# Differential attention: each group's output kept as features by queries, turned only for the squares of its norm; one more pair of key tiles as split products; split rings five deep

## The chip, the core and the metric

One core of a Trainium2 chip runs the kernel. The metric is the device time of one execution in microseconds (us). Five engines work from queues of their own and in order: PE (TensorE, matrix products and transposes; PEld is its weight load), DVE (VectorE), ACT (ScalarE), POOL (GpSimd) and SP (SyncE, which here only issues transfers). They meet at semaphores. PE writes its results to PSUM, a small memory of eight banks, each 512 numbers of four bytes wide on each of 128 partitions; DVE and ACT read it, POOL does not. SBUF is the larger on-chip memory.

## The reference

The kernel computes one layer of a diffusion backbone for two streams: 256 context tokens ("prompt", p) and 2048 latent tokens ("sample", s), 1024 wide. Per stream: a modulated norm, one projection to q, k, v and Fourier channels, differential attention in 4 heads, a Fourier mixing, an output projection with a gated residual, and a squared-ReLU MLP. What the change touches is the attention's end:

```python
s = jnp.einsum('bqhmd,bkhmd->bhmqk', qblk, k) * scale      # m: two halves of a head
p = jax.nn.softmax(s, axis=-1)
a = p[:, :, 0] - lam * p[:, :, 1]
attn = jnp.einsum('bhqk,bkhe->bqhe', a, v)                 # e: 128 features of a head
...
a = rms_norm(attn, subln_g) * (1.0 - lam_init)             # norm over the 128 features
mix = jnp.concatenate([a.reshape(b, n, 512), four], axis=-1) @ w_out
x = x + gate1 * mix
```

Sample queries see 2560 keys (512 cached and 2048 new), prompt queries their own 256. All is float32. Where a product is marked `float32r`, PE takes its operands in a shorter form; the kernel keeps the accuracy by splitting an operand into a high and a low part (`h`, `l`) and adding three products: high by high, high by low, low by high.

## The kernel before

The program has three stages that matter here, by the profile's clock: projection and Fourier mixing to about 520 us, **attention** to 1243 us, then the **output projection** to about 1470 us, and the MLP (done as seven products in place of eight, with sums of blocks) to the end.

*Attention.* Four heads, and in each head 8 groups of 256 sample queries (two blocks `j` of 128), 32 groups in all; one prompt group per head is threaded between them. The order of everything is written out: `add(t, fn)` puts a step at a nominal time, the list `ev` is sorted by time, and each engine gets its instructions in that order. Nominal time runs in slots `T` of 5 units `u`; a group takes four slots, and three groups are in flight at different depths.

- *Scores.* In each slot, five `fill`s (L1080, 2 products of 512 columns each) write five score banks `S`; DVE takes the row maximum of each (`rowmax`, L1085) and the maximum over the five (`comb`, L1088); ACT then takes five exponentials (`exp`, L1104). There are 5 `S` banks, so the fill of the next slot waits for the exponential that frees its bank.
- *Combine.* POOL forms p0 - lam * p1 (L1119, L1120), on 128 x 2560 per block.
- *Turning.* `tr` (L1135) transposes two key tiles of both blocks into one of two banks `pt`: four transposes, named by the first tile `kb` (0, 2 ... 18). ACT copies the bank to SBUF (`ah`, L1142; it is also the high part), DVE subtracts that copy from the bank (`al`, L1147; the low part). A bank `pt` is free when both have read it. Slots q = 0 to 3 of a group turn the tiles 0, 2 / 4, 6, 8 / 10, 12 / 14, 16, 18.
- *Values.* One slot later, `mul` multiplies by V into columns 0 to 255 of one bank, `po`: six split products of 256 columns per `kb` (`mm3`, L94 to L96). The tiles in `FULL`, 4 and 14, are done as plain float32 products with unsplit values instead (L1161), have no `al`, and the first quarter of tile 14 is done early (`mul_part`, L1168).
- *Output of a group.* `o1` (ACT) copies `po` columns 0 to 255 to SBUF, features by queries; `o2` (PE, L1176) transposes it into columns 256 to 511 of the same bank; `o3` (DVE, L1180) copies that to SBUF, queries by features; `o4` (ACT, L1186) takes the sums of squares; `o5` (DVE L1189, POOL L91) makes the factor of the norm; `o6` (POOL L1195) multiplies and SP stores it to `att` in DRAM, queries by features. For sample groups `o1` to `o6` stand at nominal 0, 0.4, 4.25, 8.5, 9.2 and 9.6 u after the group's last product.
- The two last groups are exceptions (`drain`, `last`): as no fills follow them, their transposes take turns over seven banks.

*Output projection.* `seq` walks 18 tiles of 128 tokens. For each, `mix` loads the attention rows (`am`), turns them back on PE (L1572, four transposes), ACT scales them with subln_g (L1573), DVE splits them (L1576, L1577), and `out_mm` does 2 x 24 products of 512 columns (L94 to L96) against the split weights from `w_split`. `finish` turns the normed result for the MLP (L248). For the first tile the turning is done at the end of the attention (`mix0_tr`, L1280).

Of the kernel before, what the change touches and what calls it, by code (L numbers as in the profile page):

```python
# [32 lines left out]
FULL = (4, 14)  # L33
# [8 lines left out]
def body(tc, a, out):  # L42
    nc = tc.nc
    ctx = ExitStack()
    with ctx:
# [16 lines left out]
        att = [scratch(f"att{i}", [P, 512]) for i in range(NT // P)]  # L62
# [46 lines left out]
        def setup_cond(pool, pps, rows):  # L109
# [8 lines left out]
            nc.vector.tensor_scalar_mul(cols[:, 96:97], cols[:, 96:97], 1.0 - LAM_INIT)  # L118
# [870 lines left out]
        with ExitStack() as c3_:  # L989
# [49 lines left out]
            class Group:  # L1039
# [66 lines left out]
                def combine(self, j):  # L1106
# [5 lines left out]
                    nc.gpsimd.tensor_scalar(self.s0e[:, j:j + 1], tot[:, 0:1], tot[:, 0:1], EPS, op0=ALU.mult, op1=ALU.mult)  # L1112
# [25 lines left out]
                def ah(self, kb):  # L1138
                    full = kb in self.hd.vf
                    t = at.tile([P, 512], F32 if full else F32R, tag="af" if full else "ah", name=f"ah{self.nm}_{kb}", bufs=2 if full else 4)  # L1140

                    (nc.vector.tensor_copy if self.drain and kb == FULL[0] else nc.scalar.copy)(t, self.pt[kb])  # L1142
                    self.A[kb] = [t]

                def al(self, kb):
                    t = at.tile([P, 512], F32R, tag="al", name=f"al{self.nm}_{kb}", bufs=4)
# [23 lines left out]
                def o1(self):  # L1170
                    self.oT = self.op.tile([P, 256], F32, tag="oT", name=f"oT{self.nm}", bufs=1 if self.last else 2)
# [6 lines left out]
                def o3(self):  # L1178
                    self.o = self.op.tile([P, 256], F32, tag="o", name=f"o{self.nm}")
                    nc.vector.tensor_copy(self.o, self.po[:, 256:512])  # L1180

                def o4(self):
                    osq = self.op.tile([P, P], F32, tag="osq", name=f"osq{self.nm}", bufs=1)
                    self.oss = self.op.tile([P, 4], F32, tag="oss", name=f"oss{self.nm}")
                    for j in range(2):
                        nc.scalar.activation(osq, self.o[:, j * P:j * P + P], AF.Square, accum_out=self.oss[:, j:j + 1])  # L1186

                def o5(self):
                    nc.vector.scalar_tensor_tensor(self.oss[:, 0:2], self.oss[:, 0:2], 1.0 / P, self.s0e, op0=ALU.mult, op1=ALU.add)  # L1189
                    pow_mhalf(self.oss[:, 2:4], self.oss[:, 0:2], 2)  # L1190

                def o6(self):
                    for j in range(2):
                        c = slice(j * P, j * P + P)
                        nc.gpsimd.tensor_scalar(self.o[:, c], self.o[:, c], self.oss[:, 2 + j:3 + j], 0.0, op0=ALU.mult, op1=ALU.add)  # L1195
                        (nc.gpsimd if self.last else nc.sync).dma_start(att[self.hd.tok0 + self.g * 2 + j][:, self.hd.hc], self.o[:, c])

            class Prompt(Group):
# [21 lines left out]
                def combine(self, j):  # L1220
# [3 lines left out]
                    nc.gpsimd.tensor_scalar(self.s0e[:, j:j + 1], t[:, 2:3], t[:, 2:3], EPS, op0=ALU.mult, op1=ALU.mult)  # L1224
# [13 lines left out]
                def mul(self, j):  # L1238

                    (ah, al), V = self.A[0], self.hd.V  # L1240
                    n = 0
                    for t in range(2):
                        c = slice((t * 2 + j) * P, (t * 2 + j) * P + P)
                        for l, r in ((ah[:, c], V[:, t, 0, :]), (ah[:, c], V[:, t, 1, :]), (al[:, c], V[:, t, 0, :])):
                            n += 1
                            nc.tensor.matmul(PRO()[:, 256 + j * P:256 + j * P + P], l, r, start=False, stop=(n == 6), skip_group_check=True)

                def o3(self):
                    self.o = self.op.tile([P, 256], F32, tag="o", name=f"o{self.nm}")
                    nc.vector.tensor_copy(self.o, PRO()[:, 256:512])  # L1250


# [8 lines left out]
            def load_wout():  # L1261
# [9 lines left out]
                MIX0.extend((f32(ts[0])[:, 2 * D:2 * D + 512], f32(ts[2])[:, 4 * D:5 * D].rearrange("p (k t) -> p k t", t=P)))  # L1271
                nc.sync.dma_start(MIX0[1][:, 4:8, :], four[:, 0:P].rearrange("(k p) t -> p k t", p=P))

            def mix0_load():
                nc.sync.dma_start(MIX0[0], att[0])

# [855 lines left out]
```

## Time and profile before

| | |
|---|---|
| median of 3 runs | 2862.73 us (2862.22 to 2862.76) |
| span of the profiled execution, first to last instruction | 2861.4 us |
| PE, DVE, ACT, POOL busy | 99%, 71%, 54%, 38% of the span |
| granted TensorE clock, mean | 0.999 |
| one group of 256 queries in the attention | about 22.0 us, start of a part to the same start of the next group |
| one tile of the output projection | 12.25 us |

The profiled execution was not timed apart from its span; its span lies 1.3 us below the median of the timed runs. In a row of the timeline stand start, length, engine, line, operation, out<-in by the program's names, shape, a count where like instructions were merged, and in brackets the idle time ahead and who ended it. PE's lengths include the way through the array, so rows overlap; the cost of a product in a dense row is the distance between starts. In a row of groups, the two numbers behind the bar are busy time in total and the mean of one in ns, then the idle time ahead and its releasers.

### The profile page before, as it was taken

The numbers are of one execution on the slowest core, as the hardware profiler recorded it, in microseconds if no ns is written. First come the engines' busy times: TensorE is split into PE (matmuls) and PEld (weight loads), VectorE is DVE, ScalarE is ACT, GpSimd is POOL, SyncE is SP. The second block draws the span as 40 slices with busy tenths as digits, with TensorE's granted clock in tenths as the row PEclk, the third lists the DMA queues.
The fourth block names the chain that finished last, engine by engine and source line by source line (L and its number), as shares of the span: only waits on it lengthen the run. The fifth ranks groups of instructions, "written<-read, shape, count | busy, mean of one in ns | idle before, by whom it ended". The sixth has DMA issues, their size and how long they took to land.

```text
span 2861.4 us, 43224 instructions
## 1 busy us (share of the span) xinstructions
PE 2831.7 (99%) x15109; PEld 2455.9 (86%) x15109; DVE 2018.0 (71%) x3393; ACT 1548.2 (54%) x3505; POOL 1073.3 (38%) x890
## 2 busy tenths in 40 slices
PE   8999999999999999999999999999999999999999
PEld 5888888688888888888889999999998888888887
DVE  7767886898988989864477777778775354345554
ACT  4333323798989989853356565556555332333221
POOL 1211223798999989942223333333332000000000
PEclk9999999999999999999999999999999999999999
DMA  7776777421211212036767676667747464445663
GB/s 284 219 207 198 230 213 237 172 106 38 73 71 53 106 38 99 23 124 201 242 221 232 223 246 228 221 219 238 234 167 255 147 202 135 138 144 185 206 206 111
DMA packets 392780, 492.94 MB, mean 172 GB/s; under 512 B 26467, under 2 KB 306384, under 8 KB 389490
## 3 DMA queue, kind: packets, MB, share of 16 engines
q1 hardware_dynamic: 387136, 479.73, 50.9%
q0 software_dynamic: 1872, 7.28, 0.8%
q10 hardware_dynamic: 3554, 3.17, 0.4%
q8 instruction: 119, 1.95, 0.3%
q14 instruction: 99, 0.81, 0.1%
HBM read 312.58 MB, written 179.59 MB: 172 GB/s over the span
## 4 chain that ended last, share of the span: by engine, by line
PE 54%; DVE 1%; DMA 0%; ACT 0%; issue 0%; SPq 0%; POOL 0%; DVEq 0%; POOLq 0%
PE ps L94 8%; PE ps L95 8%; PE ps L96 8%; PE pB L1749 2%; PE pB L1747 2%; PE pB L1748 2%; PE pA L1748 2%; PE pC L1748 2%; PE pA L1749 2%; PE pC L1747 2%; PE pA L1747 2%; PE pC L1749 2%; PE po L94 2%; PE po L96 2%; PE po L95 2%; PE pD L1749 1%
## 5 line engine op out<-in xcount | busy, mean ns | idle before, releaser
L1085 DVE TENSOR_REDUCE mxs<-Ss 128x1 f32<-128x512 f32 x636 | 405.4, 686 | 65.5 <-PE Ss L1080 55.1
L1420 DVE TENSOR_TENSOR sl<-sr,sh 128x768 fp32r<-128x768 f32 x168 | 161.8, 964 | 331.5 <-ACT sh L1419 331.1
L1120 POOL TENSOR_TENSOR P0s<-P0s,P1s 128x1024 f32<-128x1024 f32 (+2 forms) x128 | 378.6, 2958 | 10.7
L1419 ACT CAST sh<-sr 128x768 fp32r<-128x768 f32 x168 | 140.6, 838 | 418.3 <-PE ps L95 418.3
L1789 POOL TENSOR_TENSOR gs<-g,g 128x384 f32<-128x384 f32 x48 | 69.7, 1452 | 468.5 <-ACT g L1759 418.9
L1104 ACT ACTIVATE P1s<-Ss,mxs 128x512 f32<-128x512 f32 x318 | 215.4, 694 | 36.3 <-DVE mxs L1088 35.3
L94 PE MATMUL pj<-wh,hh 128*128 128x512 f32 x576 | 228.8, 397 | 2.0 <-DVE hh L555 2.0
L94 PE MATMUL ps<-thT,sh 128*128 128x512 f32 x585 | 227.6, 389 | 0.0
L95 PE MATMUL ps<-tlT,sh 128*128 128x512 f32 x585 | 227.6, 389 | 0.0
L96 PE MATMUL ps<-thT,sl 128*128 128x512 f32 x585 | 227.6, 389 | 0.0
L95 PE MATMUL pj<-wl,hh 128*128 128x512 f32 x576 | 227.1, 394 | 0.5 <-DVE wl L516 0.5
L96 PE MATMUL pj<-wh,hl 128*128 128x512 f32 x576 | 225.6, 392 | 0.0
L1104 ACT ACTIVATE P0s<-Ss,mxs 128x512 f32<-128x512 f32 x318 | 214.3, 691 | 5.6 <-DVE mxs L1088 5.0
L1135 PE MATMUL pts<-ident,P0s 128*128 128x128 f32 x1280 | 191.7, 273 | 4.5 <-DVE als L1147 1.8
L1080 PE MATMUL Ss<-KS0s,Qs 128*128 128x512 f32 x636 | 190.1, 419 | 0.4 <-ACT P1s L1104 0.4
L1080 PE MATMUL Ss<-KS1s,Qs 128*128 128x512 f32 x636 | 188.7, 420 | 1.5 <-ACT P0s L1104 1.4
L1758 ACT ACTIVATE g<-uz 128x384 f32<-128x384 f32 x144 | 75.7, 526 | 200.2 <-DVE uz L1781 174.1
L1135 PEld LDWEIGHTS pts<-ident,P0s 128*128 128x128 f32 x1280 | 151.3, 140 | 35.9 <-issue 4.8
L1119 POOL TENSOR_SCALAR P1s<-P1s,tots 128x1024 f32<-128x1024 f32 (+2 forms) x128 | 171.9, 1343 | 5.8
L1147 DVE TENSOR_TENSOR als<-pts,ahs 128x512 fp32r<-128x512 f32 x256 | 165.9, 681 | 6.9 <-ACT ahs L1142 6.7
L94 PE MATMUL ps<-ophT,sh 128*128 128x512 f32 x423 | 164.7, 389 | 1.1 <-DVE uz L1781 1.1
L96 PE MATMUL ps<-ophT,sl 128*128 128x512 f32 x423 | 164.6, 389 | 0.0
(536 smaller groups left out, 8073.9 us busy)
## 6 DMA issues: line engine op xcount, KB each, us to landing
sr<-sd SPq DMA_DIRECT2D x84, 768.0 KB, 4.5
a<-in_w SPq DMA_DIRECT2D x184, 256.0 KB, 4.2
sd<-gs SPq DMA_DIRECT2D x192, 192.0 KB, 1.9
sd<-g SPq DMA_DIRECT2D x144, 192.0 KB, 2.1
wm<-in_w_mod SPq DMA_DIRECT2D x32, 512.0 KB, 5.2
Qs<-qd SPq DMA_DIRECT2D x32, 512.0 KB, 4.0
b<-in_w SPq DMA_DIRECT2D x64, 256.0 KB, 5.8
b<-tsum SPq DMA_DIRECT2D x64, 256.0 KB, 4.7
```

Source lines behind the costliest of these rows:

```text
L94: nc.tensor.matmul(ps, lh, rh, start=first, stop=False)
L95: nc.tensor.matmul(ps, lh, rl, start=False, stop=False)
L96: nc.tensor.matmul(ps, ll, rh, start=False, stop=last)
L1080: nc.tensor.matmul(S[:, :w], self.Q[:, x, m, j * P:j * P + P], self.hd.KS[m][:, b * 512:b * 512 + w], start=(x == 0), stop=(x == 1))
L1085: nc.vector.tensor_reduce(self.mx[j][:, m, b:b + 1], self.S[j, m, b], axis=AX.X, op=ALU.max)
L1104: nc.scalar.activation(dst, S, AF.Exp, bias=self.mx[j][:, m, 6:7], accum_out=self.sm[j][:, m, b:b + 1])
L1119: nc.gpsimd.tensor_scalar(p, p, tot[:, 3:4], 0.0, op0=ALU.mult, op1=ALU.add)
L1120: nc.gpsimd.tensor_add(d, d, p)
L1135: nc.tensor.transpose(pt[:, c:c + P], self.p0[j][:, (kb + t) * P:(kb + t + 1) * P], ident)
L1747: nc.tensor.matmul(ps, wh[:, c], hh[:, k, :], start=first and k == 0, stop=False, skip_group_check=True)
L1748: nc.tensor.matmul(ps, wh[:, c], hl[:, k, :], start=False, stop=False, skip_group_check=True)
L1749: nc.tensor.matmul(ps, wl[:, c], hh[:, k, :], start=False, stop=k == 3, skip_group_check=True)
```

## The change

- Key tile 14 leaves `FULL`. It is now turned, copied and split like the others: `al(14)` is new on DVE, at 4.1 u of its slot, and six split products take the place of the float32 ones; `mul_part` is gone. The rings of `ah` and `al` have five buffers in place of four.
- The group's output stays features by queries. `o3` is gone. `o4` takes the squares from columns 256 to 511 of `po` itself. `o5` runs on POOL alone. `o6` stores the 2 x 128 factors to DRAM (`rsd`), `o7` loads them back spread over all partitions (`rb`), `o8` (POOL) multiplies, `o9` stores 128 features x 256 queries to `att`, which now has features as rows.
- A prompt group's values are formed with V as the weights, 6 products of 256 columns in place of 12 of 128; they get their own copy on ACT (`o1`), two transposes into a bank `pt` (`o2`) and squares from there (`o4`).
- `mix` needs no transposes and no ACT pass: `mT` is loaded in its final layout. The scale by subln_g moves into `w_split`, and a factor sqrt(128) with it.

```diff
-FULL = (4, 14)
+FULL = (4,)
...
-        att = [scratch(f"att{i}", [P, 512]) for i in range(NT // P)]
+        att = [scratch(f"att{i}", [512, 2 * P]) for i in range(NT // 256)]
+        rsd = [scratch(f"rs{h}", [NT // 256, 256]) for h in range(H)]
...
-name=f"ah{self.nm}_{kb}", bufs=2 if full else 4)
+name=f"ah{self.nm}_{kb}", bufs=1 if full else 5)
...
-                def o3(self):
-                    self.o = self.op.tile([P, 256], F32, tag="o", name=f"o{self.nm}")
-                    nc.vector.tensor_copy(self.o, self.po[:, 256:512])
...
-                        nc.scalar.activation(osq, self.o[:, j * P:j * P + P], AF.Square, accum_out=self.oss[:, j:j + 1])
+                        nc.scalar.activation(osq, self.po[:, 256 + j * P:256 + j * P + P], AF.Square, accum_out=self.oss[:, j:j + 1])
 
                 def o5(self):
-                    nc.vector.scalar_tensor_tensor(self.oss[:, 0:2], self.oss[:, 0:2], 1.0 / P, self.s0e, op0=ALU.mult, op1=ALU.add)
+                    nc.gpsimd.tensor_add(self.oss[:, 0:2], self.oss[:, 0:2], self.s0e)
                     pow_mhalf(self.oss[:, 2:4], self.oss[:, 0:2], 2)
 
+                def place(self):
+                    return nc.gpsimd if self.last else nc.sync, self.hd.tok0 // 2 + self.g
+
                 def o6(self):
-                    for j in range(2):
-                        c = slice(j * P, j * P + P)
-                        nc.gpsimd.tensor_scalar(self.o[:, c], self.o[:, c], self.oss[:, 2 + j:3 + j], 0.0, op0=ALU.mult, op1=ALU.add)
-                        (nc.gpsimd if self.last else nc.sync).dma_start(att[self.hd.tok0 + self.g * 2 + j][:, self.hd.hc], self.o[:, c])
+                    q, n = self.place()
+                    q.dma_start(rsd[self.hd.h][n].rearrange("(p j) -> p j", j=2), self.oss[:, 2:4])
+
+                def o7(self):
+                    q, n = self.place()
+                    self.rb = self.op.tile([P, 256], F32, tag="P0_1" if self.hd.s else "rb", name=f"rb{self.nm}", bufs=2 if self.hd.s else 1)
+                    q.dma_start(self.rb, rsd[self.hd.h][n:n + 1].partition_broadcast(P).rearrange("p o d -> p (o d)"))
+
+                def o8(self):
+                    q, n = self.place()
+                    v = self.oT.rearrange("p (j t) -> p j t", j=2)
+                    nc.gpsimd.tensor_mul(v, v, self.rb.rearrange("p (t j) -> p j t", j=2))
+
+                def o9(self):
+                    q, n = self.place()
+                    q.dma_start(att[n][self.hd.hc], self.oT)
...
-                for t, fn, *args in ((0.25, gp.tr, 0), (0.9, gp.ah), (1.4, gp.al), (15.4, gp.mul, 0), (17.0, gp.mul, 1),
-                                     (20.85, gp.o3), (39.5, gp.o4), (40.2, gp.o5), (40.6, gp.o6)):
-                    add(G[5] + (t - 5 if h == H - 1 and t > 30 else t) * u, fn, *args)
+                for t, fn, *args in ((0.25, gp.tr, 0), (0.9, gp.ah), (1.4, gp.al), (17.0, gp.mul), (20.85, gp.o1), (24.2, gp.o2),
+                                     (24.9, gp.o4), (25.6, gp.o5), (28.2, gp.o6), (32.7, gp.o7),
+                                     (40.2, gp.o8), (43.0, gp.o9)):
+                    add(G[5] + t * u, fn, *args)
...
-                            tr_t, ah_t, al_t = [0.7, 2.2, 3.86], [3.3, 3.8, 4.4], [None, 4.6, 5.2]
+                            tr_t, ah_t, al_t = [0.7, 2.2, 3.86], [3.3, 3.8, 4.4], [4.1 if q == 3 else None, 4.6, 5.2]
...
-                            if q == 3 and not n:
+                            if kb in FULL and q == 3:
                                 add(w + 3.95 * u, gr.mul_part, kb)
...
-                    for t, fn in ((0, gr.o1), (0.4, gr.o2), (0.75 if gr.last else 4.25, gr.o3), (8.5, gr.o4), (9.2, gr.o5), (9.6, gr.o6)):
+                    for t, fn in ((0, gr.o1), (0.4, gr.o2), (8.5, gr.o4), (9.2, gr.o5), (11.8, gr.o6), (16.3, gr.o7), (23.4, gr.o8), (26.0, gr.o9)):
...
             def mix(i):
-                    am, mT = M[i]
-                    pm = PRO().rearrange("p (k t) -> p k t", t=P)
-                    for k in range(4):
-                        nc.tensor.transpose(pm[:, k, :], am[:, k * P:k * P + P], ident)
-                    nc.scalar.activation(mT[:, 0:4, :], pm, AF.Copy, scale=cols[:, 96:97])
+                mT = MIX0[0] if i == s0 else M[i]
```

Three places show how instructions stand. In the names, `s1_1_18` is sample, head 1, group 1, key tile 18, and the number behind is the buffer; `Ss1_3_1_0_4` is the fifth score bank of a slot. A row ends with the engines it waits for.

On PE, at the end of slot q = 3 of group 1 of head 1, the turning of tile 18 stands between the last fill of the slot and the products of tiles 10 and 12. Before:

```order
L1080 MATMUL Ss1_3_1_0_4_8433<-KS0s1_6065,Qs1_3_8022 128x512 [waits Activation_49]
L1080 MATMUL Ss1_3_1_0_4_8433<-KS0s1_6065,Qs1_3_8022 128x512
L1135 MATMUL pts1_1_18_8438<-ident_175,P0s1_1_0_7721 128x128 [waits Activation_49]
L1135 MATMUL pts1_1_18_8438<-ident_175,P0s1_1_1_7872 128x128
L1135 MATMUL pts1_1_18_8438<-ident_175,P0s1_1_0_7721 128x128
L1135 MATMUL pts1_1_18_8438<-ident_175,P0s1_1_1_7872 128x128
L94 MATMUL po_5307<-ahs1_1_10_8358,Vs1_6369 128x256
```

The same place of the changed kernel (its lines are one higher):

```order
L1081 MATMUL Ss1_3_1_0_4_8454<-KS0s1_6059,Qs1_3_8041 128x512 [waits Activation_49]
L1081 MATMUL Ss1_3_1_0_4_8454<-KS0s1_6059,Qs1_3_8041 128x512
L1136 MATMUL pts1_1_18_8459<-ident_170,P0s1_1_0_7738 128x128 [waits DVE_49,PE_49]
L1136 MATMUL pts1_1_18_8459<-ident_170,P0s1_1_1_7886 128x128
L1136 MATMUL pts1_1_18_8459<-ident_170,P0s1_1_0_7738 128x128
L1136 MATMUL pts1_1_18_8459<-ident_170,P0s1_1_1_7886 128x128
L95 MATMUL po_5302<-ahs1_1_10_8382,Vs1_6367 128x256
```

The order on PE is the same; what moved is the wait. Tile 18 takes the bank of tile 14, which was free after ACT's copy and is now free after DVE's `al(14)`.

On DVE, at the same time, where that `al` stands. Before:

```order
L1085 TENSOR_REDUCE mxs1_3_1_8403<-Ss1_3_1_0_3_8427 128x1 [waits PE_49]
L1085 TENSOR_REDUCE mxs1_3_1_8403<-Ss1_3_1_0_4_8433 128x1 [waits PE_49]
L1088 TENSOR_REDUCE mxs1_3_1_8403<-mxs1_3_1_8403 128x1 [waits DVE_49]
L1147 TENSOR_TENSOR als1_1_16_8460<-pts1_1_16_8420,ahs1_1_16_8436 128x512 [waits Activation_49]
L1147 TENSOR_TENSOR als1_1_18_8464<-pts1_1_18_8438,ahs1_1_18_8457 128x512 [waits Activation_49]
```

And in the changed kernel:

```order
L1086 TENSOR_REDUCE mxs1_3_1_8423<-Ss1_3_1_0_3_8447 128x1 [waits PE_49]
L1086 TENSOR_REDUCE mxs1_3_1_8423<-Ss1_3_1_0_4_8454 128x1 [waits PE_49]
L1148 TENSOR_TENSOR als1_1_14_8477<-pts1_1_14_8418,ahs1_1_14_8452 128x512 [waits Activation_49]
L1089 TENSOR_REDUCE mxs1_3_1_8423<-mxs1_3_1_8423 128x1 [waits DVE_49]
L1148 TENSOR_TENSOR als1_1_16_8482<-pts1_1_16_8440,ahs1_1_16_8457 128x512 [waits Activation_49]
L1148 TENSOR_TENSOR als1_1_18_8486<-pts1_1_18_8459,ahs1_1_18_8479 128x512 [waits Activation_49]
```

The new `al(14)` stands behind the row maximum of the slot's fifth score bank, and ahead of the maximum over the five for which ACT waits.

On ACT, the squares (`osqs`) of group 1 stand one slot later, between the copies of tiles 10 and 12 of group 2 and the exponentials of the next scores. Before:

```order
L1104 ACTIVATE P0s1_4_0_8615,sms1_4_0_8549<-Ss1_4_0_0_4_8587,mxs1_4_0_8548 128x512
L1142 CAST ahs1_2_10_8662<-pts1_2_10_8625 128x512 [waits PE_49,Activation_49]
L1142 CAST ahs1_2_12_8667<-pts1_2_12_8651 128x512 [waits PE_49,Activation_49]
L1186 ACTIVATE osqs1_1_8684,osss1_1_8685<-os1_1_8619 128x128 [waits DVE_49]
L1186 ACTIVATE osqs1_1_8684,osss1_1_8685<-os1_1_8619 128x128 [waits Activation_49]
L1104 ACTIVATE P1s1_4_0_0_8691,sms1_4_0_8549<-Ss1_4_0_1_0_8630,mxs1_4_0_8548 128x512 [waits DVE_49,Pool_49]
```

And in the changed kernel:

```order
L1105 ACTIVATE P0s1_4_0_8644,sms1_4_0_8577<-Ss1_4_0_0_4_8615,mxs1_4_0_8576 128x512
L1143 CAST ahs1_2_10_8690<-pts1_2_10_8652 128x512 [waits PE_49,Activation_49]
L1143 CAST ahs1_2_12_8695<-pts1_2_12_8679 128x512 [waits PE_49,Activation_49]
L1183 ACTIVATE osqs1_1_8712,osss1_1_8713<-po_5302 128x128 [waits DMAHW6_49,PE_49]
L1183 ACTIVATE osqs1_1_8712,osss1_1_8713<-po_5302 128x128 [waits Activation_49]
L1105 ACTIVATE P1s1_4_0_0_8719,sms1_4_0_8577<-Ss1_4_0_1_0_8657,mxs1_4_0_8576 128x512 [waits DVE_49,Pool_49]
```

The place is the same. The squares read `po` instead of an SBUF tile, and wait for PE instead of DVE. The last product into `po` ahead of them in the program is that of tile 8 of group 2: in nominal time the products of tiles 4, 6 and 8 stand at 3.9 u of this slot, the squares at 4.5 u, the exponentials at 5 u.

73 lines of the change are left out of this document (36 added, 37 removed).

## The prediction

> **What bounds the kernel now.** First the page: the busy shares, PE over forty slices, the granted clock.
>
> ```profile
> PE 2831.7 (99%) x15109; PEld 2455.9 (86%) x15109; DVE 2018.0 (71%) x3393; ACT 1548.2 (54%) x3505; POOL 1073.3 (38%) x890
> PE   8999999999999999999999999999999999999999
> PEclk9999999999999999999999999999999999999999
> ```
>
> PE has work in every slice, at full clock. So a product taken off PE is worth its length, and a wait put in front of PE costs its length. But a busy PE is not PE at its peak, so the next view is the busy time by stage: first the attention (from the first to the last early part of tile 14), then the output projection.
>
> ```profile
> 569.00:1243.40 674.40, 671.41 (x4355) 568.27 (x4354) 594.51 (x1165) 603.69 (x1689) 612.12 (x495) 1.00 0.19 66
> 1243.40:1500.00 256.60, 253.23 (x1259) 214.53 (x1258) 152.87 (x207) 115.54 (x252) 65.44 (x59) 1.00 0.67 215
> ```
>
> The columns are the window, its length, then busy PE, PEld, DVE, ACT, POOL, the clock, DMA share and GB/s. In the attention PE idles 3.0 us of 674, while DVE, ACT and POOL stand at 88 to 91%: PE is the bound, with three engines close behind it in one ring of waits. Anything that makes one of them wait for PE, and PE for it in turn, shows at once. The timeline around the end of a slot q = 3 shows how close the ring runs (PE, then DVE, then ACT):
>
> ```profile
> 1120.68 1.19 PE L1080 MATMUL Ss<-KS0s,Qs 128*128 128x512 f32 x4
> 1121.70 0.60 PE L1135 MATMUL pts<-ident,P0s 128*128 128x128 f32 x4
> 1122.06 0.36 PE L94 MATMUL po<-ahs,Vs 128*128 128x256 f32 x1
> ...
> 1119.60 3.12 DVE L1085 TENSOR_REDUCE mxs<-Ss 128x1 f32<-128x512 f32 x5 [0.56 <-PE Ss L1080]
> 1122.75 0.16 DVE L1088 TENSOR_REDUCE mxs<-mxs 128x1 f32<-128x5 f32 x1
> 1122.83 1.28 DVE L1147 TENSOR_TENSOR als<-pts,ahs 128x512 fp32r<-128x512 f32 x2
> ...
> 1120.91 0.60 ACT L1142 COPY ahs<-pts 128x512 f32<-128x512 f32 x1
> 1122.34 0.59 ACT L1142 CAST ahs<-pts 128x512 fp32r<-128x512 f32 x1 [0.34 <-PE pts L1135]
> ```
>
> PE turns tile 18 at 1121.70, directly behind the fill. It may, because ACT copied tile 14 out of that bank by 1121.51 (1120.91 + 0.60). DVE is a full row maximum behind PE: its fifth ends at 1122.72.
>
> **Stall 1: the turning of tile 18 waits for `al(14)`.** In the changed kernel the bank is free only after `al(14)`, which stands on DVE behind that fifth maximum, and the fifth maximum needs the fill that PE has only just done. One `al` takes 0.68 us, two take 1.28, so one adds 0.60: `al(14)` ends at 1122.72 + 0.60 = 1123.32. How fast PE follows a DVE `al` stands at one place before, where a turning waited for the prompt's `alp`:
>
> ```profile
> 656.29 0.68 DVE L1235 TENSOR_TENSOR alp<-ptp,ahp 128x512 fp32r<-128x512 f32 x1
> 657.11 0.63 PE L1135 MATMUL pts<-ident,P0s 128*128 128x128 f32 x4 [0.33 <-DVE alp L1235]
> ```
>
> From 656.97 to 657.11, 0.14 us. So tile 18 is turned at 1123.46 and not at 1121.70: 1.76 us later. The fifth maximum could begin at most 0.14 us sooner (the fill ends at 1121.87, the maximum began at 1122.04), so I take 1.7, between 1.5 and 1.8. ACT's copy of tile 18, and the exponentials behind it, slide by as much, so nobody gains time to make it up. All groups but the last two (whose transposes use seven banks) have it: 30 x 1.7 = **+51**, bounds 45 and 54. What PE could do meanwhile, the products of tiles 10 and 12, stands behind the transpose in its queue. On that the Trainium skill ("TensorE: Matmul & The Clock Gate", Part 2, Step-by-step) says that PE pulls only weight loads ahead and keeps its matmuls in program order; by it the stall is whole, with free reordering it would be nil, and the 0.33 us above, with fills queued behind, agrees with the first.
>
> **Stall 2: ACT's squares wait for the products of the same slot.** The squares now read `po`. Do waits go by halves of that bank, or by the whole? The groups by line tell:
>
> ```profile
> L1161 PE MATMUL po<-ahs,vf4s 128*128 128x256 f32 x128 | 33.0, 380 | 1.1 <-DVE os L1180 1.1
> ```
>
> Here the products, which write columns 0 to 255, waited for DVE's copy of columns 256 to 511. They go by the whole. So ACT's squares wait for the last product ahead of them in the program, that of tile 8 in the same slot. Before, they ran beside these products:
>
> ```profile
> 781.54 0.35 ACT L1186 ACTIVATE osqs<-os 128x128 f32<-128x128 f32 x1
> 782.24 0.19 ACT L1186 ACTIVATION_READ_ACCUMULATOR osqs<-os 128x1 f32 x1
> 782.69 0.69 ACT L1104 ACTIVATE P1s<-Ss,mxs 128x512 f32<-128x512 f32 x1 [0.27 <-DVE mxs L1088]
> 783.37 0.68 ACT L1104 ACTIVATE P1s<-Ss,mxs 128x512 f32<-128x512 f32 x1
> ...
> 783.50 0.28 PE L96 MATMUL po<-ahs,Vs 128*128 128x256 f32 x1
> 783.62 0.60 PE L1135 MATMUL pts<-ident,P0s 128*128 128x128 f32 x4
> 783.97 1.65 PE L1080 MATMUL Ss<-KS0s,Qs 128*128 128x512 f32 x6
> 785.45 0.60 PE L1135 MATMUL pts<-ident,P0s 128*128 128x128 f32 x4
> ```
>
> The squares took 781.54 to 782.43. Now they begin when the last product has ended, 783.78, and end at 784.67; the five exponentials behind them begin there and not at 782.69, 2.0 us late. The next fill, at 783.97, needs the bank that the first of them frees, at 784.67 + 0.69 = 785.36: PE waits 1.4 us. Exponentials follow each other by 0.67 us, the three fills by 0.49 (783.97 to 785.45), so the third waits about 0.3 more: 1.75 us. In the four groups in which prompt products stand between (0.62 us, quoted below) it is 1.1. There are 29 groups with fills to follow: 25 x 1.75 + 4 x 1.1 = **+48**. Bounds: 36 (1.3 each: the first fill alone, 0.1 of it regained) and 54 (1.95: all of ACT's delay). The squares themselves from PSUM in place of SBUF I take at the same 0.89 us. The Trainium skill ("PSUM — Partial Sum Buffer", PSUM bank collisions raise a hardware error) asks that PSUM be guarded by bank and quadrant of partitions, not by address; by that rule this stall is whole, with a guard by address it would be nil, and the trace's 1.1 us wait sides with the rule.
>
> **What PE saves.** Tile 14: the early part and the rest of the float32 products, and the split ones behind.
>
> ```profile
> 766.56 0.38 PE L1168 MATMUL po<-ahs,vf14s 128*128 128x128 f32 x2
> 770.32 0.82 PE L1161 MATMUL po<-ahs,vf14s 128*128 128x128 f32 x4
> 771.09 0.28 PE L95 MATMUL po<-als,Vs 128*128 128x256 f32 x1
> 771.21 0.28 PE L96 MATMUL po<-ahs,Vs 128*128 128x256 f32 x1
> ```
>
> The early part is two passes of 0.11 (0.38 less 0.27, the length of one), 0.22. The rest, from 770.32 to 771.09 less one product of 0.115, is 0.655. Six split products in their place are 0.69. So 0.18 less, x 32 = **-5.8**. The new `al` is 0.68 us of DVE, but `o3` (0.41) and DVE's part of `o5` go, and DVE has 80 us idle in the stage: the cost is in its place, not its length.
>
> Output projection, the four transposes of one tile between products:
>
> ```profile
> 1263.14 0.39 PE L96 MATMUL po<-woh,ml 128*128 128x512 f32 x1
> 1263.37 0.60 PE L1572 MATMUL po<-ident,am 128*128 128x128 f32 x4
> 1264.04 0.40 PE L95 MATMUL po<-wol,mh 128*128 128x512 f32 x1
> 1271.02 1.09 PE L248 MATMUL ptb<-ident,xn 128*128 128x128 f32 x8 [1.56 <-DVE xn L235]
> ```
>
> From L96 to the second product behind, 0.90; without transposes it is two steps of 0.23. That is 0.44 for each of 17 tiles, 7.5; `mix0_tr` adds 0.4, and one 0.44 is lost at 1271.02, where PE waits for DVE anyway: **-7.5**, bounds -5 and -8.5. `mT` comes in its layout by the same kind of load as its Fourier half did; ACT's pass goes, and it bounded nothing.
>
> Prompt groups: twelve products go, six come, and the squares move ahead of a slot's exponentials.
>
> ```profile
> 671.80 0.34 PE L1246 MATMUL po<-Vp,ahp 128*128 128x128 f32 x2
> ...
> 672.42 0.62 PE L1135 MATMUL pts<-ident,P0s 128*128 128x128 f32 x4
> ...
> 771.63 0.69 ACT L1104 ACTIVATE P1s<-Ss,mxs 128x512 f32<-128x512 f32 x1 [0.55 <-DVE mxs L1088]
> ```
>
> Half of the twelve take 0.62, all 1.24; six of 256 columns 0.69. Two transposes add about 0.3. They stand behind the slot's products (done at 772.4 in that slot), so ACT's squares wait for them until 772.8, and the exponentials start at 773.7 and not at 771.63: a third stall of some 1.5 us by the sum above, once a head. 4 x (1.5 + 0.3 - 0.55), **+5**, bounds 0 and 8.
>
> **Sum.** 2861.4 + 51 + 48 - 5.8 - 7.5 + 5 = 2952.1 for the profiled execution; the median of the runs stood 1.3 above its span, so **2953**. Its own bounds: 2861 + 45 + 36 - 5.8 - 8.5 - 3 (PE's idle 3.0 us, if all is absorbed) = 2925, and + 54 + 54 + 8 - 5.8 - 5 + 10 for what POOL may add (below), 2977.
>
> **The rivals.**
>
> *No stall, faster.* If `al(14)` ended before PE wants its bank, and the squares found PE's products done, only the savings are left: 2861.4 - 5.8 - 7.5 - 1 + 1.3 = 2848. It decides at 1121.70: `al(14)` would have to end 1.76 us sooner than the rows allow, before the fill it stands behind. For it speaks only that DVE loses 0.4 us and more of other work; against it the order. 0.06.
>
> *One stall only.* Were the squares' wait for an earlier product, stall 1 alone gives 2861.4 + 51 - 13.3 + 3 = 2902 (0.08); were tile 18's wait covered, stall 2 alone gives 2899 (0.05).
>
> *POOL becomes late.* The factors now go to DRAM and back before POOL multiplies, and a POOL that waits holds up the combine that stands behind.
>
> ```profile
> att<-os SPq DMA_DIRECT2D x62, 64.0 KB, 1.6
> Vs<-vd SPq DMA_DIRECT2D x4, 2560.0 KB, 8.8
> ```
>
> A small store took 1.6 us, and store and load have 4.5 u and 7.1 u of room, so two in a row fit; behind a head's loads of K and V (8.8 us) one may come some 2 us late. POOL idles 62 us in the stage, 2 us a group, and two stalls give it 3 more. With ten such delays of 3 us past that cover: 2983. 0.04.
>
> **How the numbers follow.** Forecast 0.75, one stall 0.13, POOL late 0.04, no stall 0.06, and 0.02 for something near no change. The range reaches down to the single stalls and up a little past the own bounds: 2895 to 2982. Within 0.2% counts as no change, about what a measurement of this kernel can tell. Slower 0.92, same 0.02, faster 0.06.
>
> **What would show it.** Right: in the attention PE's idle time grows from 3 to about 100 us; the turning of tile 18 is released by DVE's `al` some 1.7 us after the fill; ACT's squares by PE's product, with about 1.4 us of idle time ahead of the next fill, released by the exponential. A group takes 25.3 us and not 22.0; a tile of the output projection 11.8 and not 12.25. Wrong: if ACT's squares begin in the midst of the products, if the five maxima run closer to the fills than before, or if POOL waits for `rb`.

## The result, and the profile after

The changed kernel takes **2959.84 us** (median of 4 runs, 2959.14 to 2960.43) against 2862.55 us (2862.22 to 2862.76): ratio 1.034, 95% interval 1.0327 to 1.0354. Slower by 97 us, where 2953 was forecast. Its profiled execution has a span of 2957.3 us, 95.9 more than before, at a granted clock of 0.998.

The page of the changed kernel, the same three rows:

```profile
PE 2841.2 (96%) x15021; PEld 2438.8 (82%) x15021; DVE 2003.0 (68%) x3353; ACT 1532.3 (52%) x3491; POOL 1073.7 (36%) x891
PE   8999999898888888889999999999999999999999
PEclk9999999999999999999999999999999999999999
```

The nines of the attention have become eights; the clock has not moved. Its busy times by stage (columns as before; the attention now ends near 1340):

```profile
569.00:1340.00 771.00, 684.93 (x4312) 554.78 (x4311) 586.74 (x1125) 596.79 (x1689) 615.64 (x493) 1.00 0.25 62
1340.00:1600.00 260.00, 254.75 (x1251) 216.41 (x1251) 150.64 (x216) 111.96 (x250) 64.42 (x64) 0.99 0.72 220
```

PE idles 86 us of the attention, not 3. POOL does as much as before, DVE and ACT a little less: the time is not work, it is waiting. The view of waits in that stage says for whom (us in total, times, longest):

```profile
POOL tots L1112 <- DVE tots L1111: 98.9, 30, 4.3
...
ACT osqs L1183 <- PE po L97: 63.7, 30, 2.3
...
PE pts L1136 <- DVE mxs L1089: 46.7, 29, 1.6
PE Ss L1081 <- ACT P1s L1105: 34.5, 32, 1.2
```

The timeline at the turning of tile 18, where PE went on without a gap before (PE, then DVE):

```profile
1157.15 0.63 PE L1081 MATMUL Ss<-KS0s,Qs 128*128 128x512 f32 x2
1159.39 0.63 PE L1136 MATMUL pts<-ident,P0s 128*128 128x128 f32 x4 [1.61 <-DVE mxs L1089]
...
1157.35 1.29 DVE L1086 TENSOR_REDUCE mxs<-Ss 128x1 f32<-128x512 f32 x2 [0.21 <-PE Ss L1081]
1158.56 0.68 DVE L1148 TENSOR_TENSOR als<-pts,ahs 128x512 fp32r<-128x512 f32 x1
1159.16 0.15 DVE L1089 TENSOR_REDUCE mxs<-mxs 128x1 f32<-128x5 f32 x1
```

`al(14)` ends at 1159.24, PE turns at 1159.39. Back to back it would have been 1157.64 (two products of the fill at 0.245 each): 1.75 us. The row names the maximum over the five, which ends in the same moment; run e7 shows that `al(14)` is meant. The timeline at the squares, ACT and then PE:

```profile
867.08 0.28 ACT L1183 ACTIVATE osqs<-po 128x128 f32<-128x128 f32 x1 [2.17 <-PE po L97]
...
867.65 0.19 ACT L1183 ACTIVATION_READ_ACCUMULATOR osqs<-po 128x1 f32 x1
867.75 0.68 ACT L1105 ACTIVATE P1s<-Ss,mxs 128x512 f32<-128x512 f32 x1
...
866.76 0.28 PE L97 MATMUL po<-ahs,Vs 128*128 128x256 f32 x1
866.88 0.60 PE L1136 MATMUL pts<-ident,P0s 128*128 128x128 f32 x4
868.57 2.07 PE L1081 MATMUL Ss<-KS0s,Qs 128*128 128x512 f32 x6 [1.09 <-ACT P1s L1105]
```

ACT stands 2.17 us before the squares, until PE's last product (866.76 + 0.28) is out. The fill could have started 0.35 behind the turning's start, as at 783.97 before, so at 867.23. It did at 868.57, and its six products take 2.07 us where they took 1.65: 1.34 + 0.42 = 1.76 us. Only 1.09 of it is shown as idle; the rest is inside "busy" rows that are spread out, so the wait rows (46.7 + 34.5 us) hold less than the stalls cost.

So that the runs can be compared stage by stage, the span of each profiled execution is cut at four starts in its trace: the first and the last `fill`, the first and the last product of the output projection. All in us.

| kernel | median | fills | to first output product | output projection | behind it |
|---|---|---|---|---|---|
| before | 2862.6 | 698.6 | 28.1 | 222.1 | 1394.1 |
| after | 2959.8 | 799.2 | 30.6 | 213.9 | 1395.0 |
| e1, squares from a copy | 2911.9 | 749.7 | 31.3 | 214.5 | 1395.8 |
| e2, tile 14 unsplit | 2911.4 | 752.2 | 29.9 | 214.5 | 1395.3 |
| e3, both | 2864.8 | 701.5 | 30.6 | 217.3 | 1395.5 |
| e4, before with squares from `po` | 2915.2 | 747.1 | 33.3 | 222.1 | 1394.5 |
| e11, before with tile 14 split | 2915.8 | 749.1 | 30.4 | 223.1 | 1394.3 |
| e7, `al(14)` one place up | 2893.5 | 731.4 | 32.1 | 214.2 | 1395.3 |
| e6, order mended | 2899.8 | 735.9 | 31.4 | 215.4 | 1396.2 |
| e9, squares from `po` earlier | 2866.8 | 705.7 | 30.0 | 214.5 | 1395.3 |
| e5, e3 and prompt's squares late | 2866.6 | 698.3 | 35.1 | 217.5 | 1395.3 |
| e8, e6 and prompt's squares late | 2900.4 | 735.7 | 33.9 | 217.6 | 1395.3 |
| e10, e5 and tile 2 first | 2867.0 | 698.8 | 33.1 | 219.9 | 1395.3 |
| e12, e10 and the queue cleared | 2861.4 | 698.2 | 27.9 | 217.3 | 1395.0 |

After against before: +100.6 in the fills, +2.5 at their end, -8.2 in the output projection, +0.9 behind. The stages of a row are those of one execution and the median is of all: e12's profiled execution is the fastest of its eleven (2857.7), those of e4 (2917.7), e8 (2902.1) and e11 (2919.6) are the slowest of their four, and in some a granted clock of about 0.8 for 10 to 20 us moves a stage by 1 to 3 us.

### The profile page after: what moved, and what is told of

It reads as the page before. It is cut to its first block, busy times and chain, and to the rows that moved or that the text cites. A ratio compares the mean times of both kernels' runs of the same rounds, so it can differ in the third digit from the quotient of the medians.

```text
span 2957.3 us, 43041 instructions
## 1 busy us (share of the span) xinstructions
PE 2841.2 (96%) x15021; PEld 2438.8 (82%) x15021; DVE 2003.0 (68%) x3353; ACT 1532.3 (52%) x3491; POOL 1073.7 (36%) x891
## 4 chain that ended last, share of the span: by engine, by line
PE 52%; DVE 1%; issue 0%; ACT 0%; POOL 0%; DVEq 0%
PE ps L95 8%; PE ps L97 8%; PE ps L96 8%; PE pB L1754 2%; PE pB L1753 2%; PE pB L1755 2%; PE pC L1754 2%; PE pA L1753 2%; PE pA L1754 2%; PE pC L1755 2%; PE pC L1753 2%; PE pA L1755 2%; PE po L97 2%; PE po L95 2%; PE po L96 2%; PE pD L1755 1%
## 5 line engine op out<-in xcount | busy, mean ns | idle before, releaser
L1081 PE MATMUL Ss<-KS0s,Qs 128*128 128x512 f32 x636 | 201.5, 429 | 34.9 <-ACT P1s L1105 34.9
L1105 ACT ACTIVATE P1s<-Ss,mxs 128x512 f32<-128x512 f32 x318 | 214.9, 696 | 23.8 <-DVE mxs L1089 21.5
L1105 ACT ACTIVATE P0s<-Ss,mxs 128x512 f32<-128x512 f32 x318 | 214.5, 695 | 4.1 <-DVE mxs L1089 4.0
L1148 DVE TENSOR_TENSOR als<-pts,ahs 128x512 fp32r<-128x512 f32 x288 | 187.6, 682 | 30.4 <-ACT ahs L1143 30.3
L1143 ACT CAST ahs<-pts 128x512 fp32r<-128x512 f32 x288 | 162.9, 613 | 79.5 <-PE pts L1136 79.5
L95 PE MATMUL po<-ahs,Vs 128*128 128x256 f32 x576 | 172.1, 299 | 0.0
```

The source lines that it names most:

```text
L95: nc.tensor.matmul(ps, lh, rh, start=first, stop=False)
L1081: nc.tensor.matmul(S[:, :w], self.Q[:, x, m, j * P:j * P + P], self.hd.KS[m][:, b * 512:b * 512 + w], start=(x == 0), stop=(x == 1))
L1105: nc.scalar.activation(dst, S, AF.Exp, bias=self.mx[j][:, m, 6:7], accum_out=self.sm[j][:, m, b:b + 1])
L1148: nc.vector.tensor_sub(t, self.pt[kb], f32(self.A[kb][0]))
```

## The experiments

**e1 to e4: each stall undone, both undone, one made in the kernel before.** Theory: the two stalls are separate and together the whole loss. Rivals: the squares are late because of the factors' way through DRAM; the turning waits for the fifth maximum anyway; the stalls share their time.

e1 puts DVE's copy back for the squares:

```diff
+                def o3(self):
+                    if not self.last:
+                        self.o = at.tile([P, 256], F32, tag="o", ...)
+                        nc.vector.tensor_copy(self.o, self.po[:, 256:512])
...
-                        nc.scalar.activation(osq, self.po[:, 256 + j * P:256 + j * P + P], AF.Square, ...)
+                        o = self.po[:, 256:512] if self.last else self.o
+                        nc.scalar.activation(osq, o[:, j * P:j * P + P], AF.Square, ...)
...
-(0.4, gr.o2), (8.5, gr.o4)
+(0.4, gr.o2), (0.75 if gr.last else 4.25, gr.o3), (8.5, gr.o4)
```

> The changed kernel, but DVE again copies the turned output out of po (o3) and ACT takes the squares from that copy; oT has two buffers in place of three, to make room; tile 14 stays split. Theory (ACT's squares in po wait for the products of the same slot, 25 x 1.75 + 4 x 1.1 = 48 us): 2960 - 48 = 2912, up to 2925 if only the 34.9 us count that PE's rows of the fill show; ACT's squares are no longer released by PE, and the turning of tile 18 still waits 1.6 us a group. Rival A (the squares are late for another reason, the factors' way through DRAM holding their buffer): 2960, squares still late. Rival B (the two stalls share their time, so that one alone costs nearly what both cost): 2945 or more.

Measured: 2911.9 us (ratio to before 1.0173, 1.0157 to 1.0188). 47.9 gained. PE's waits in the attention, longest first:

```profile
PE pts L1136 <- DVE mxs L1089: 46.5, 29, 1.6
PE po L1177 <- ACT oTs L1173: 2.8, 5, 1.8
PE Ss L1081 <- ACT P1s L1105: 2.5, 3, 0.9
```

The wait at the fill is gone, that of the turning stands as it was.

e2 undoes the split of tile 14 alone:

```diff
-FULL = (4,)
+FULL = (4, 14)
...
-[4.1 if q == 3 else None, 4.6, 5.2]
+[None, 4.6, 5.2]
```

> The changed kernel, but tile 14 is back among the unsplit tiles (no al(14), float32 products with the early quarter, rings of four and af of two); squares stay in po. Theory (al(14) behind the fifth row maximum holds the turning of tile 18 for 1.6 us in 30 groups): 2960 - 48 to 51 + 5.8 = 2915 to 2918, no wait of the turning on DVE above 0.2 us a group. Rival A (the turning is held by the fifth row maximum or the maximum over the five, whatever al does): 2960 to 2966. Rival B (the stalls share their time): 2945 or more.

Measured: 2911.4 us (1.0173, 1.0158 to 1.0188). 48.4 gained, 4 to 7 more than worked out. PE's waits:

```profile
PE Ss L1081 <- ACT P1s L1105: 34.7, 32, 1.2
PE po L1177 <- ACT oTs L1173: 3.0, 6, 1.8
```

Now the turning waits no more, and the fill does. e3 has both edits:

> The changed kernel with both undone: squares from DVE's copy, tile 14 unsplit. What is left of the change is the output kept as features, the factors' way through DRAM, the prompt's new order and the output projection without transposes. Theory (the stalls are separate and add, the rest is -8.2 in the output projection and about +5 for the prompt): 2858 to 2864, against 2862.6 before. Rival (a third cost is in what is left: POOL waiting for rb, or DVE and POOL losing time to the new loads): 2875 or more, with PE idle in every group and not once a head.

Measured: 2864.8 us (1.0008, 0.9998 to 1.0018), 1 above the theory's upper end and 10 under the rival's 2875. One more stall undone gains 47.1 (from e1) and 46.6 (from e2), as much as alone: the stalls add and share nothing. An ordinary group takes 21.98 us in before and e3, 23.55 in e1, 23.8 in e2 and 25.3 in after; 1.57 + 1.82 = 3.4, against the 3.3 of the whole.

e4 makes stall 2 in the kernel before; the copy stays there for the multiplication:

```diff
-activation(osq, self.o[:, j * P:j * P + P], ...)
+o = self.o if self.hd.s or self.last else self.po[:, 256:512]
+activation(osq, o[:, j * P:j * P + P], ...)
```

> The kernel before, with one edit: the squares of sample groups are taken from po in place of DVE's copy, which stays for the multiplication. Theory (the wait on po is the whole of stall 2): 2862.6 + 48 = 2911, bounds 36 to 54 more, so 2899 to 2917; from PE's rows of after 35, 2898. PE waits in the next slot's first fill for the exponential. Rival (what made the squares late is the new order around them or the factors' way through DRAM): 2863 to 2868.

Measured: 2915.2 us (1.0186, 1.0171 to 1.0201), +52.6. In the profiled execution the fills take 48.5 more and the end of the last groups 5.3; there the granted clock was 0.77 and 0.89 in two stretches of 10 us (1276 to 1296), and 1.00 at the same place in before, so part of the 5.3 is not the squares'. The operand of the squares alone makes the stall, with the rest of the change absent.

**e11: tile 14 split in the kernel before**, the same lines the other way round, with the rings of five.

> The kernel before with one edit: tile 14 split (al(14) behind the fifth row maximum, six split products, rings of five). Theory (stall 1 less what the split products save, as undoing it showed twice: 48.4 and 47.1 us): 2862.6 + 47 = 2910, the turning of tile 18 waiting 1.6 us on DVE in 30 groups. Rival (the stall needs the rest of the change, o3 gone from DVE and the factors on POOL): 2885 or less.

Measured: 2915.8 us (1.0186, 1.0172 to 1.0199), +52.6, against +47 expected; 50.5 in the fills. PE's longest wait:

```profile
PE pts L1135 <- DVE mxs L1088: 49.0, 30, 1.8
```

The stall does not need the rest of the change. The profiled execution is 3.7 us above the median; its first fill comes 2.4 us later than in before, though the two kernels do not differ ahead of it, and its second group takes 20.8 us and not 19.8 at a granted clock of 0.83 (540 to 550 us). So 1.0 of the 3.5 us by which its fills exceed the 47 is that stretch; the rest of the difference stays open.

**e7: one DVE instruction, one place up** (on e1). If PE waits for the work ahead of `al(14)` on DVE, moving it ahead of the fifth maximum takes one maximum off the wait.

```diff
-al_t = ... [4.1 if q == 3 else None, 4.6, 5.2]
+al_t = ... [3.8 if q == 3 and 1 < 8 * h + g < 30 else ..., 4.6, 5.2]
```

> The kernel with the squares from DVE's copy and tile 14 split, with one instruction moved by one place in 28 groups: al(14) stands ahead of the fifth row maximum and not behind it. Theory (the turning of tile 18 waits as long as the maxima ahead of al(14) take): it waits 1.6 - 0.64 = 1.0 us; 2911.9 - 28 x 0.64 = 2894. Rival A (the wait is for the maximum over the five, or for the fifth one): 2911 to 2915. Rival B (the fifth maximum, now 0.64 later, holds up the exponentials and the next fill by as much as the turning gains): 2905 to 2915, with PE waiting at the fill for ACT.

Measured: 2893.5 us (1.0109, 1.0094 to 1.0124). PE's longest wait:

```profile
PE pts L1136 <- DVE als L1148: 28.2, 28, 1.0
```

From 1.61 to 1.0 us, and now the row names `al` itself. Rival A would have left the time as it was.

**e6: the split tile kept, its order mended.** Besides, tile 18 is turned behind the products of tiles 10 and 12 and copied behind the second exponential. The edit leaves out the fifth group of each head (`g != 4`), so it holds for 24 groups and not for the 28 of the expectation; the four others keep the order of e1:

```diff
+                        if q == 3 and g != 4 and 1 < 8 * h + g < 30:
+                            tr_t, ah_t, al_t = [0.7, 2.2, 3.95], [3.3, 3.8, 5.9], [3.8, 4.6, 6.4]
```

> As the one before (squares from DVE's copy, tile 14 split, al(14) ahead of the fifth maximum), and besides tile 18 is turned behind the products of tiles 10 and 12 in place of ahead of them, and ACT copies it behind the second exponential of the next slot (28 groups). Theory (PE has 1.4 us of products to do while al(14) ends, so the wait is covered and the 0.18 us a group of tile 14 are gained): 2864.8 - 5 = 2860, up to 2878 if the fifth maximum, 0.64 us later, delays the next fill by the whole of that. Rival (the ring has no room for a split tile 14 in that slot, DVE and ACT being at 90%): 2890 or more, with a new wait of the second turning of the next slot for al(18).

Measured: 2899.8 us (1.0128, 1.0113 to 1.0144). A miss: more than e7, 22 above the theory's upper end, and in the rival's range. Where the edit holds, the long wait is gone, and short ones stand in its place (PE's waits in the attention; of the five waits of 1.6 us, four are in the fifth groups):

```profile
PE Ss L1081 <- ACT P0s L1105: 11.3, 24, 0.7
PE pts L1136 <- DVE mxs L1089: 8.0, 5, 1.6
PE pts L1136 <- DVE tots L1110: 5.7, 10, 0.6
PE pts L1136 <- DVE als L1148: 4.7, 14, 0.4
```

The timeline of one such place, DVE, ACT, PE:

```profile
1131.99 0.68 DVE L1148 TENSOR_TENSOR als<-pts,ahs 128x512 fp32r<-128x512 f32 x1
1132.59 0.68 DVE L1086 TENSOR_REDUCE mxs<-Ss 128x1 f32<-128x512 f32 x1
1133.30 0.16 DVE L1089 TENSOR_REDUCE mxs<-mxs 128x1 f32<-128x5 f32 x1
...
1133.58 0.69 ACT L1105 ACTIVATE P0s<-Ss,mxs 128x512 f32<-128x512 f32 x1 [1.63 <-PE pts L1136]
...
1134.92 0.59 ACT L1143 CAST ahs<-pts 128x512 fp32r<-128x512 f32 x1
...
1133.05 0.60 PE L1136 MATMUL pts<-ident,P0s 128*128 128x128 f32 x4
...
1136.23 0.50 PE L1081 MATMUL Ss<-KS1s,Qs 128*128 128x512 f32 x1 [0.42 <-ACT P0s L1105]
```

ACT stands idle 1.63 us. Its exponential waits for two engines. One is DVE: the fifth maximum, pushed back by `al(14)`, is combined at 1133.46. The other is PE: the exponential overwrites the buffer of `P0` (there are five) that tile 18 is still turned from, and the third of the four transposes, the last to read it, is out at 1133.54, 0.04 ahead of the exponential. So the moved turning has become late as well, as late as the maximum. Then ACT has the copy of tile 18 (0.59) between its exponentials, and a fill waits for the next one. A group takes 23.0 us, 1.0 more than in e3. In the three orders tried (e1, e7, e6), the split tile made a group 1.6, 1.0 and 1.0 us longer than in e3, with what its products save already in it. How much of the 1.0 in e6 is the late maximum, the late turning or the late copy was not tried.

**e9: the squares still from `po`, 1.8 u earlier** (on e2). On ACT they then stand ahead of the slot's copies, when nothing is pending on `po`.

```diff
-(8.5, gr.o4), (9.2, gr.o5)
+(6.7, gr.o4), (9.2, gr.o5)
```

> The changed kernel with tile 14 unsplit, and the squares still read from po, but at 6.7 u in place of 8.5: on ACT behind the fifth exponential of the slot and ahead of its copies of turned tiles, while PE's products into po of that slot are still to come. Theory (stall 2 is the place, not the reading of po: there nothing is pending on po, and the squares end about 1 us ahead of the products): 2862 to 2870, as with DVE's copy (2864.8), against 2911.4 with the squares at 8.5 u. Rival A (reading po costs wherever it stands, since PE's products then wait for ACT): 2890 or more, with PE's products released by ACT's squares. Rival B (ACT's copies, 0.9 us later, hold up the ring): 2875 or more, with PE's turning or fill released by ACT.

Measured: 2866.8 us (1.0012, 1.0002 to 1.0021), 44.6 less than e2 with one number changed. The intervals of e9 and e3 overlap, but a weight load of the products now waits for the squares, in the view of waits:

```profile
PEld po L1162 <- ACT osqs L1183: 10.2, 31, 0.4
```

That is 0.33 us a group, and a group takes 22.18 us and not the 21.98 of e3. So reading `po` is nearly free; the place was the stall. It is also the same guard seen from the other side: products that write columns 0 to 255 wait for squares that read 256 to 511. That is as the Trainium skill ("PSUM — Partial Sum Buffer", PSUM bank collisions raise a hardware error) has it, which asks for a guard by bank and quadrant of partitions, not by address.

**e5, e8: the prompt's squares from a copy, behind a slot's exponentials** (e5 on e3, e8 on e6), with DVE's copy at 25.3 u, the squares at 29.5 in place of 24.9, and the steps behind them 4.6 u later.

> The kernel with both stalls undone, and in it the prompt's squares moved: DVE copies the two turned blocks out of the bank pt (25.3 u), ACT takes the squares from that copy behind a slot's exponentials (29.5 u), and the steps behind them move by 4.6 u. Theory (the third stall, 1.55 us once a head: the group that holds it takes 24.7 and not 23.15 us): 2864.8 - 6 = 2859, and that group at 23.1 to 23.3 us. Rival (the group is long because of the two turnings and the new products, not the squares): 2864 to 2866, the group at 24.5 us or more.

Measured: 2866.6 us (1.0013, 1.0004 to 1.0023): a miss. From first fill to first fill, the group in question takes 23.2 us and not 24.7, but the next one 22.5 and not 21.85, so 0.9 of the 1.55 was the squares. The fills are 3.2 us shorter (in the fourth head the prompt's squares come behind the last fill), and the first output product comes 4.5 us later behind them.

> Both of the mended orders in one: tile 14 split with tile 18 turned behind the products, and the prompt's squares late. Theory (the two are in different slots and add): 6 us below the run with the mended order alone, so about 2854, which is 0.3% below the kernel before. Rival (no room): 2885 or more.

Measured: 2900.4 us (1.0131, 1.0114 to 1.0148): nothing gained on e6. The prompt's gain is there, about 1 us in each of three heads (the three groups around the squares take 72.5 us, in e6 73.4 to 73.6). The fills show none of it (735.7 us, 735.9 in e6), as the second group takes 22.2 us and not 19.8, at a granted clock of 0.83 from 540 to 560 us, where e6 has 1.00. And the first output product comes 2.5 us later.

**e10, e12: where that gain went.** In e5, PE waits 6.9 us for the first tile's rows, which come from the last head's prompt, through its factors. e10 lets the output projection begin with tile 2, stored long before:

```diff
-seq = [i + s * NTH for i in range(NTH) for s in range(2)]
+seq = [i + s * NTH for i in (2, 0, 1, *range(3, NTH)) for s in range(2)]
```

> The kernel with both stalls undone and the prompt's squares late, and the output projection walks its tiles in another order: tile 2 first (queries of the first sample group, stored long before) and tiles 0 and 1 behind, so that the first tile's attention rows do not come from the prompt of the last head. Theory (the 3 us that the late squares gain are lost again where PE waits 6.9 us for the first tile, whose rows hang on the chain of factors through DRAM): 2866.5 - 6.9 = 2859.6, first product of the output projection 28 us behind the last fill and not 35. Rival (the weights' split or the last group holds that product as well): 2863 to 2867.

Measured: 2867.0 us (1.0014, 1.0005 to 1.0022): a miss. The first output product comes 2.0 us sooner, but PE still waits 4.96 us there, and the first tile takes 19.0 us where it took 16.6. SP's part of the timeline shows why:

```profile
1242.02 0.32 SPq L1205 DMA_DIRECT2D rbs<-rs  x1
1242.44 0.37 SPq L1214 DMA_DIRECT2D att<-oTp  x1
1242.86 0.43 SPq L1305 DMA_DIRECT2D wout<-att  x1
1248.18 0.32 SPq L1214 DMA_DIRECT2D att<-oTs  x1
1249.53 0.32 SPq L1200 DMA_DIRECT2D rs<-osss  x1
1249.90 0.43 SPq L1585 DMA_DIRECT2D mT<-att  x1
```

The load of tile 2 (`wout<-att`) needs nothing of the prompt, but it stands in SP's queue behind the prompt's store (`att<-oTp`), and the next tile's (`mT<-att`) behind the seventh group's factors. e12 issues the first load 14 slots earlier (not 8, as the expectation has it; at 1167.93 and not at 1242.86) and takes those stores off SP:

```diff
-return nc.gpsimd if self.last else nc.sync, ...
+return nc.gpsimd if self.last or self.drain else nc.sync, ...
...
+                    if self.hd.h == H - 1 and (self.hd.s or self.g == 5):
+                        q = nc.gpsimd
                     q.dma_start(att[n][self.hd.hc], self.oT)
...
-            add(base + (AVS - 2) * T + 0.7 * u, mix0_load)
+            add(base - 10 * T + 0.7 * u, mix0_load)
```

> As the one before (both stalls undone, the prompt's squares late, tile 2 first), and the queue ahead of the first tiles' loads is cleared: the load of tile 2's attention rows is issued 8 slots earlier, and of the last head the stores of the prompt's and the sixth group's output, and the factors and the store of the seventh group, go through POOL's queue and not SP's. Theory (not the data but SP's order held the first tile: its load stood behind the prompt's store, tile 11's behind the seventh group's factors; PE waited 5.0, 2.4 and 0.5 us there): 2867.0 - 7.5 = 2859.5, with the first product of the output projection 29 us behind the last fill and not 33. Rival (the weights' split on ACT and DVE, or the queue of POOL, holds these products): 2864 or more.

Measured: 2861.4 us, 2857.7 to 2864.8 in 11 runs, where before had 2860.9 to 2863.1; ratio 0.9999, 0.999 to 1.0008. Why these runs differ more stays open. SP in the same stretch:

```profile
1241.16 0.32 SPq L1205 DMA_DIRECT2D rbs<-rs  x1
1241.65 0.37 SPq L1587 DMA_DIRECT2D mT<-att  x1
```

The first output product comes 27.9 us behind the last fill and not 33.1: SP's order it was, though the earlier load and the moved stores were not tried apart. PE's waits of 5.0 and 2.4 us for the first two tiles are down to one of 1.5. This is the best version found, and it is no faster than the kernel before.

Its output projection still takes 217 us, as in e3 and e5, where e1, e2 and e9 take 214.5. The difference lies in the first tiles, as from the fourth on each takes 11.77 us in all of them: the first takes 13.4 to 13.6 us in e1, e2 and e9, 16.5 in e3, 16.6 in e5 and 19.0 in e10, and in e12 the first three take 13.6, 13.8 and 13.5. Part of it is waits for data, and part the granted clock: in the first two stretches of 10 us of that stage it was 0.83 and 1.00 in e1, 0.83 and 0.83 in e5, 0.71 and 0.83 in e10; in e12 it was 1.00 there and 0.88 and 0.94 in the next two. So the end of the attention costs more than the distance to the first product shows.

## Why the prediction was right

1. *PE bounds the attention, and a wait put in front of it costs its length.* Right. An ordinary group takes 25.3 us, as foretold. Idle time came out at 86 us where about 100 was foretold, because part of a stall lies inside spread-out rows. The terms of the attention add up to 51 + 48 - 5.8 + 5 = 98, and the fills took 100.6 more.
2. *Stall 1, 1.7 us a group.* Right in mechanism and size: 1.75 from start to start, `al(14)` to PE 0.15 us where 0.14 was taken from the prompt's `alp`. Net of tile 14's saving the sum had 45 us; undoing it gained 48.4 and 47.1, and making it in before cost 52.6. In an ordinary group it is 1.57 = 1.75 - 0.18, which fits the saving of 0.18; the saving was not measured by itself.
3. *Stall 2, 1.75 us a group.* Right: 1.34 for the first fill and 0.42 for those behind, where 1.4 and 0.3 were forecast. Undone it gained 47.9 and 46.6, against 48. One part was off and did no harm: two squares from `po` take 0.76 us (867.08 to 867.84), not the 0.89 that they took from SBUF. The sign "ACT's squares released by PE's product" came as foretold, 30 times.
4. *Output projection, -7.5.* Measured -8.2; a tile takes 11.77 us, not 12.25.
5. *Prompt groups, +5.* Right in sum, off in its parts. The three groups around the prompt's squares take 1.2, 0.9 and 1.4 us more in e3 than in before in the first three heads, where 1.25 a head was forecast; in the fourth they fall behind the last fill. The third stall is there, but moving the squares (e5) gave back 1.1, 0.8 and 0.9 us and not 1.5. So that term was too large; what remains in e5 over before, for which the sum had 0.3 - 0.55, is +0.1, +0.1 and +0.5.
6. *What the sum left out.* The first output product comes 2.5 us later behind the last fill. The change also issues the load of the first tile's rows three slots later (`mix0_load`, nominal base + 4 T and not base + T), which the sum has no term for. The forecast looked for POOL waiting for the factors in the midst of the attention. It came at its end, where nothing covers it. There, on the kernel with the prompt's squares late, other data for the first tile took 2.0 us off that distance (e5 to e10), SP's order 5.2 (e10 to e12); on the changed kernel itself it was not tried.
7. *The rivals.* "No stall" and "one stall only" are what e3, e1 and e2 show when the stalls are taken away. "POOL becomes late" holds for the last groups: in the changed kernel POOL waits for the factors 0.7 and 0.4 us in the midst of the attention, and 6.5, 12.6 and 2.8 us at its end.

## What to carry to other kernels

A new reader of a shared buffer costs little by its own length; look at what stands ahead of it on its in-order engine, and at which pending writer it now has to wait for, since here one number in the order of ACT was worth 45 us. Where a ring of engines is close to full, as here with three of them at 88 to 91%, a short instruction inside the loop (fill, maximum, exponential, fill) can cost PE more than its length: `al(14)` takes 0.68 us, and a group became about 1 us or more longer in each of the three orders tried. A wait that names one engine may hide another that ended in the same moment; what an instruction overwrites counts as much as what it reads. A result that is sent through DRAM and back is hidden while there is other work; at the end of a stage its stores stand ahead of the next stage's loads in the same queue.

## What the runs showed of the hardware

- ACT squared 128 x 128 from PSUM in 0.28 us (after), from SBUF in 0.31 to 0.36 (before).
- A store of 1 KB in 8-byte pieces was slow for its size. In e10, SP issued the prompt's factors and the load that reads them 3.9 us apart (3.2 in e12), and nothing between; the load waits until the store has landed:

```profile
1233.31 0.32 SPq L1200 DMA_DIRECT2D rs<-ossp  x1
1237.23 0.32 SPq L1205 DMA_DIRECT2D rbp<-rs  x1
```

The stores of 64 KB before the change took 1.6 us from issue to landing (median of 62).
